# Indexer and top-k ahead of the state space mixer, and the mixer's scan done by scan instructions

## The chip, the cores and the metric

The program runs on one core of a Trainium2 chip. The metric is the device time of one execution in microseconds (us). The engines of the core work independently and wait for each other by semaphores: TensorE (PE, matmuls), VectorE (DVE), ScalarE (ACT), GpSimd (POOL) and SyncE (SP, which issues transfers).

## The reference

The program is one layer with two blocks over 512 positions of width 1024, in fp32. The change is in the first block. It projects the normed input, runs a state space mixer on one half and a sparse attention on the other, and joins them with a gated residual:

```python
def first_block(...):
    mod = silu(c) @ w_ada + b_ada
    shift, scale, gate = split(mod, 3)
    h = rms_norm(x, norm_g) * (1 + scale) + shift
    ssm_u, ssm_z, q, k, v, attn_z, q_idx, k_idx, w_idx = split(h @ w_in)
    y_ssm = s5_mixer(ssm_u, ...) * silu(ssm_z)
    y_attn = dsa_mixer(q, k, v, q_idx, k_idx, w_idx, ...) * silu(attn_z)
    return x + gate * (concat([y_ssm, y_attn]) @ w_out)

def s5_mixer(u, ...):                  # per group of 16 channels, 64 complex states
    lam_bar = exp(lam * dt)
    bu = einsum('gpc,bsgc->bsgp', b_bar, ug)
    states = associative_scan(s_t = lam_bar * s_(t-1) + bu_t)
    y = einsum('gcp,bsgp->bsgc', c_mat, states).real + d_skip * u

def dsa_mixer(q, k, v, q_idx, k_idx, w_idx, ...):
    score = sum over 8 heads of w_idx * relu(q_idx . k_idx), causal
    keep the 128 best keys of each query, attend to them with softmax
```

## The kernel before

All products of fp32 matrices are made from two parts, a rounded one and its rest. ScalarE casts a weight chunk (`whi`, L145), VectorE subtracts to get the rest (`wlo`, L146), and TensorE makes three matmuls (L153, L154, L155). Intermediate tiles of 128x512 come from one ring of 49 buffers, so that a tile's first write waits until the tile that had the buffer before is done with.

TensorE and SP run in the order of the code. The orders of VectorE, ScalarE and GpSimd are set by a scheduler. Two work streams are woven on TensorE: a main stream says after each step how many microseconds of other work it wants beside it, and `weave` (L230) draws that much from a fill stream of projections. `alongside` runs several streams by their asked times, `both` runs them one after the other, `hold(t)` only asks for t.

The stretch that the change rebuilds runs from about 70 us to about 294 us, and has two weaves (L693 and L694). In the first, the main stream is the position bias table, the tables of the state space mixer (`ssm_tables`: powers of the transition, the input matrices `Bb` and `BP`), `ssm_back` (L1201 to L1206, the output matrices F, four quarters of real and imaginary part, 24 GpSimd instructions of 128x512), `ssm_taps` (L1224 and L1225, eight groups of small matmuls, which give `We` and the tap matrix KK) and `ssm_scan`. The fill begins with the indexer's projection: four chains of 24 matmuls with 384 columns, each of which writes two tiles that VectorE splits (`iq`, L887), then the projections of queries, keys, values and the attention's gate (`ga`, L687).

`ssm_scan` works on chunks of 8 positions. 64 pairs of small matmuls (L1243) give the chunks' inputs, ScalarE copies them to `Str` and `Sti` (L1245), and then GpSimd walks the chunks: 7 steps over 16x8 chunk states at once, 7 steps over 16, 7 steps over 16x7, each of 8 instructions (L1256 to L1263), 168 in all. Beside it eight transfers put KK into the matrix `TO`, which GpSimd has cleared before (L1215).

In the second weave the index scores are made (24 pairs of matmuls, L943 and L944, relu on ScalarE, sums on VectorE at L948 and L950) and the top-k masks (48 rounds on VectorE, L966 and L967); after a hold of 40 the bias is turned (L932) and `ssm_out` makes the mixer's output in 32 groups (L1289 with `TO`, then L1291 with F and `Str`, `Sti`, all of 64 columns); after a hold of 44 `gate_sums` multiplies the 16 chunks of the gate's weights on GpSimd (`wadag`, L902), sums them on ScalarE (L903) and adds the parts on VectorE (L905, L906). The attention follows; its first TensorE work is the transposes of the keys `kn`.

Of the kernel before, what the change touches and what calls it, by code (L numbers as in the profile page):

```python
# [8 lines left out]
F32 = mybir.dt.float32  # L9
# [3 lines left out]
OP = mybir.AluOpType  # L13
# [91 lines left out]
class Kern:  # L105
# [342 lines left out]
    def block1(self):  # L448
# [235 lines left out]
        def ev_ga(j, p):  # L684
# [118 lines left out]
        self.resid(y, A["w_out"], lambda: self.gate, A["xT"], self.col("attn_norm"), (0, 1, 4, 5, 2, 6, 3, 7))  # L803
# [88 lines left out]
    def gate_sums(self):  # L892
# [4 lines left out]
        for j in range(8):  # L897
# [6 lines left out]
            yield 1.5  # L904
        nc.vector.tensor_tensor(out=self.gate, in0=part[:, 0], in1=part[:, 1], op=OP.add)  # L905
        nc.vector.tensor_tensor(out=self.gate, in0=self.gate, in1=self.col("b_ada")[:, 16:24], op=OP.add)  # L906

# [194 lines left out]
    def ssm_tables(self):  # L1102
# [6 lines left out]
        Q = [mk("q8" + x, (128, 8, 16)) for x in "ri"]  # L1109
# [25 lines left out]
        def powers(v, one, rev):  # L1135

            at = lambda e, n: [x[:, one - e - n + 1:one - e + 1] if rev else x[:, one + e:one + e + n] for x in v]
# [26 lines left out]
        yield from self.abreast(powers(PW, 7, 1), coef())  # L1164
# [3 lines left out]
        for x in range(2):  # L1168
            nc.vector.tensor_copy(Q[x][:, 0, :], PW[x][:, 0, :])
        self.Q = Q  # L1170
# [4 lines left out]
        yield from self.abreast(powers(Q, 0, 0), self.cmul(nc.vector, Bb[0], Bb[1], kb, B, tb))  # L1175
# [10 lines left out]
        self.BP = BP  # L1186

    def ssm_back(self):
# [19 lines left out]
        yield 0.0  # L1208

    def ssm_taps(self):  # L1210
# [3 lines left out]
        self.TO = TO = big.tile([128, 8, 16, 32], F32, name="TO", tag="TO", bufs=1)  # L1214
        nc.gpsimd.memset(TO.rearrange("p a b c -> p (a b c)"), 0.0)  # L1215
# [17 lines left out]
    def ssm_scan(self):  # L1233
        nc, big = self.nc, self.sp
# [598 lines left out]
```

## Time and profile before

| | before |
|---|---|
| median of 3 runs | 1275.62 us (1275.29 to 1276.29) |
| the profiled execution | 1278.79 us |
| its span, first to last instruction | 1277.0 us |
| TensorE busy | 1199.1 us (94%) |
| VectorE busy | 828.2 us (65%) |
| ScalarE busy | 558.1 us (44%) |
| GpSimd busy | 473.0 us (37%) |
| mean granted TensorE clock | 0.952 |

The profile shows one execution. Times in the trace count from the start of the span. A line such as "L146" is a line of the kernel. "PE ps_t L1291 <- POOL Str L1259: 6.6, 1, 6.6" is read: TensorE's instruction of line 1291 waited 6.6 us in all, once, and what released it was GpSimd's instruction of line 1259 that wrote `Str`. The granted clock is given as a share of full speed: 1.00 is 2.4 GHz, 0.50 is 1.2 GHz. A duration of a matmul includes its way through the array, so the distance from one start to the next is its cost in a dense stretch.

### The profile page before, as it was taken

How to read it: one execution, taken by the hardware profiler on the slowest of the kernel's cores; microseconds unless marked ns; L12 is line 12 of the kernel's file. 1: busy time of each engine (PE TensorE's matmuls, PEld its weight loads, DVE VectorE, ACT ScalarE, POOL GpSimd, SP SyncE). 2: the span in 40 equal slices, each digit the busy share in tenths (PEclk: the TensorE clock that was granted, in tenths of full speed). 3: DMA queues.
4: the chain of work that ended last, by engine and by line, in shares of the span. 5: the costliest groups of instructions: out<-in, count | busy, mean ns of one | idle time of the engine just before them, and what ended most of it. 6: DMA issues, size and time to landing. Idle time of an engine off the chain costs nothing.

```text
span 1277.0 us, 17205 instructions
## 1 busy us (share of the span) xinstructions
PE 1199.1 (94%) x6264; PEld 980.0 (77%) x6264; DVE 828.2 (65%) x1603; ACT 558.1 (44%) x1053; POOL 473.0 (37%) x612
## 2 busy tenths in 40 slices
PE   2687997999799999998999999999999999999998
PEld 2477996887578998987777777688888888888876
DVE  7986699827765456786767575554577743577731
ACT  4333542326673443655665555423544421344420
POOL 3569799517742027245666565201000000000000
PEclk9795998559999999999999999999999999999999
DMA  9442224123125442232111101134332223333230
GB/s 352 138 139 78 71 71 153 58 62 120 34 66 193 147 120 61 67 100 64 37 33 51 33 34 34 50 100 148 99 99 86 92 91 95 99 92 89 95 112 33
DMA packets 113908, 118.06 MB, mean 92 GB/s; under 512 B 16312, under 2 KB 101344, under 8 KB 113824
## 3 DMA queue, kind: packets, MB, share of 16 engines
q1 hardware_dynamic: 101280, 103.00, 25.5%
q10 hardware_dynamic: 12544, 13.96, 3.4%
q8 instruction: 49, 0.80, 0.3%
q14 instruction: 35, 0.29, 0.1%
HBM read 109.47 MB, written 6.30 MB: 91 GB/s over the span
## 4 chain that ended last, share of the span: by engine, by line
PE 74%; POOL 8%; DVE 5%; issue 3%; ACT 1%; POOLq 0%; DVEq 0%; ACTq 0%
PE ps_g L153 19%; PE ps_g L154 18%; PE ps_g L155 18%; PE ps_t L369 4%; PE ps_o L383 4%; PE ps_t L1291 3%; PE ps_s L342 2%; PE ps_s L341 2%; PE ps_t L1289 1%; DVE rb L1550 1%; POOL Sti L1263 1%; PE ps_o L1625 1%; POOL sm L1257 1%; POOL Str L1259 1%; POOL sm L1261 1%
## 5 line engine op out<-in xcount | busy, mean ns | idle before, releaser
L146 DVE TENSOR_TENSOR wlo<-wraw,whi 128x1024 fp32r<-128x1024 f32 (+4 forms) x143 | 195.6, 1373 | 71.4 <-ACT whi L145 71.2
L145 ACT CAST whi<-wraw 128x1024 fp32r<-128x1024 f32 (+4 forms) x161 | 161.7, 1010 | 175.2 <-PE ps_g L154 152.5
L153 PE MATMUL ps_g<-hT,whi 128*128 128x512 f32 x504 | 206.8, 410 | 0.0
L155 PE MATMUL ps_g<-hT,wlo 128*128 128x512 f32 x504 | 198.9, 395 | 0.0
L154 PE MATMUL ps_g<-hT,whi 128*128 128x512 f32 x504 | 198.7, 394 | 0.0
L350 POOL TENSOR_TENSOR P<-P,rsum 128x256 f32<-128x256 f32 (+3 forms) x144 | 100.8, 730 | 76.7 <-DVE rsum L1412 31.3
L345 ACT ACTIVATE P<-P,nm 128x128 f32<-128x128 f32 (+3 forms) x160 | 89.7, 561 | 75.2 <-DVE nm L343 74.2
L153 PEld LDWEIGHTS ps_g<-hT,whi 128*128 128x128 f32 x504 | 95.3, 189 | 26.9 <-issue 9.3
L155 PEld LDWEIGHTS ps_g<-hT,wlo 128*128 128x128 f32 x504 | 94.9, 188 | 22.1
L154 PEld LDWEIGHTS ps_g<-hT,whi 128*128 128x128 f32 x504 | 95.3, 189 | 18.7 <-issue 1.2
L343 DVE CUSTOM_DVE_ANT_0 P<-ps_s,att 128x128 f32<-128x128 f32 (+3 forms) x128 | 62.1, 485 | 50.9 <-PE ps_t L369 27.5
L369 PE MATMUL ps_t<-consts,P 128*128 128x128 f32 x400 | 66.1, 279 | 10.5 <-DVE qst L890 6.1
L153 PE MATMUL ps_g<-act,whi 128*128 128x512 f32 (+1 forms) x176 | 71.0, 404 | 0.0
L155 PE MATMUL ps_g<-act,wlo 128*128 128x512 f32 (+1 forms) x176 | 69.4, 394 | 0.0
L154 PE MATMUL ps_g<-act,whi 128*128 128x512 f32 (+1 forms) x176 | 69.4, 394 | 0.0
L850 POOL TENSOR_TENSOR acc<-acc,sq 128x512 f32<-128x512 f32 x15 | 21.9, 1461 | 122.1 <-ACT sq L849 119.0
L369 PEld LDWEIGHTS ps_t<-consts,P 128*128 128x128 f32 x400 | 46.7, 141 | 26.5 <-issue 14.7
L154 PE MATMUL ps_g<-wlo,hT 128*128 128x256 f32 (+1 forms) x208 | 59.3, 285 | 2.0 <-DVE wlo L146 2.0
L153 PE MATMUL ps_g<-whi,hTh 128*128 128x256 f32 x192 | 59.5, 310 | 1.3 <-ACT V L673 1.3
L153 PE MATMUL ps_g<-whi,hT 128*128 128x256 f32 (+1 forms) x208 | 59.4, 286 | 1.3 <-ACT sq L1327 1.3
L155 PE MATMUL ps_g<-whi,hT 128*128 128x256 f32 (+1 forms) x208 | 59.2, 285 | 0.0
L1739 DVE TENSOR_TENSOR conv<-ps_g,R 128x512 f32<-128x512 f32 x43 | 29.7, 692 | 43.8 <-PE ps_g L155 43.8
(487 smaller groups left out, 3031.4 us busy)
## 6 DMA issues: line engine op xcount, KB each, us to landing
wraw<-in_w_in_dram SPq DMA_DIRECT2D x56, 512.0 KB, 3.5
wraw<-in_w_up_dram SPq DMA_DIRECT2D x40, 512.0 KB, 3.5
wada<-in_w_ada_dram SPq DMA_DIRECT2D x16, 512.0 KB, 7.5
wraw<-in_w_down_dram SPq DMA_DIRECT2D x16, 512.0 KB, 3.3
wadag<-in_w_ada_dram ACTq DMA_DIRECT2D x16, 256.0 KB, 3.4
wraw<-in_w_out_dram SPq DMA_DIRECT2D x8, 512.0 KB, 3.3
wraw<-in_w_attn_br_dram SPq DMA_DIRECT2D x8, 512.0 KB, 3.3
wraw<-in_w_o_dram SPq DMA_DIRECT2D x8, 512.0 KB, 3.4
```

The lines of the kernel that those rows point to most:

```text
L145: nc.scalar.copy(hi, src)
L146: (eng or nc.vector).tensor_tensor(out=lo, in0=src, in1=hi, op=OP.subtract)
L153: mm(out, lhsT=l[0], rhs=r[0], start=start, stop=False)
L154: mm(out, lhsT=l[0], rhs=r[1], start=False, stop=False)
L155: mm(out, lhsT=l[1], rhs=r[0], start=False, stop=stop)
L343: nc.vector.tensor_tensor_reduce(out=P[i], in0=s, in1=madd(i), scale=-1.0, scalar=3.0e38, op0=OP.add, op1=OP.min, accum_out=nm[:, i:i + 1])
L345: nc.scalar.activation(P[i], P[i], AF.Exp, scale=-1.0, bias=nm[:, i:i + 1], accum_out=sums[:, i:i + 1])
L350: nc.gpsimd.tensor_tensor(out=P[n], in0=P[n], in1=sc[:, n:n + 1].to_broadcast([128, (n + 1) * 128]), op=OP.mult)
L369: nc.tensor.transpose(pt[:, o:o + 128], P[i][:, j * 128:(j + 1) * 128], self.ident)
L383: nc.tensor.matmul(acc[x * 64:(x + 1) * 64, j * 128:], lhsT=V(j), rhs=tiles[b][:, o:o + w], start=start and j == 0, stop=stop and j == 2)
L1291: nc.tensor.matmul(o, lhsT=self.F[x][a // 4][s, a % 4 * 128:(a % 4 + 1) * 128], rhs=self.St[x][s, a, 0:64], start=False, stop=x == 1)
L1739: TT(out=u, in0=p, in1=R[0], op=OP.mult)
```

## The change

The indexer alone is now the fill of the first weave, whose main stream is the bias table and the mixer's tables. The second weave starts the index scores at once, by rows of queries from the shortest on (first all heads with 256 keys, then 384, then 512), followed by the top-k; beside it stand `ssm_taps` and `ssm_scan` after a hold of 2, and after a hold of 26 more the bias and `ssm_out`.

The scan's recurrence is turned by the phase of each state, so that what is left is a real decay: GpSimd turns the inputs (12 instructions of 128x512 for two halves), VectorE runs four scan instructions of 128x512 (L1297), and GpSimd turns back (12 more). The tables for this, `turn` and `keep`, are made on GpSimd behind `BP` by six doublings with a small correction each; the power table Q on VectorE is gone. `ssm_back`, the clearing of `TO` and its eight transfers stand behind the scan now. The two additions of the gate sum are made where the residual uses the gate.

```diff
-        fill = self.both(indexer(), proj(1024, qf), proj(1536, kf), self.gemm_tn(hT, 8, w_in, 2048, 512, ev_v),
+        fill = self.both(proj(1024, qf), proj(1536, kf), self.gemm_tn(hT, 8, w_in, 2048, 512, ev_v),
...
-        self.weave(self.both(self.bias_table(), self.alongside(ssm_chunks(), tables), self.ssm_back(), self.ssm_taps(), self.ssm_scan()), fill, left=True)
+        self.weave(self.both(self.bias_table(), self.alongside(ssm_chunks(), tables)), indexer())
         self.weave(self.alongside(self.both(self.index_scores(iq, kk, wi, score), self.top_mask(score, sel)),
-                                  self.both(self.hold(40.0), self.bias_flip(), self.ssm_out(z)), self.both(self.hold(44.0), self.gate_sums())), fill, left=True)
+                                  self.both(self.hold(2.0), self.ssm_taps(), self.ssm_scan(), self.hold(26.0), self.bias_flip(), self.ssm_out(z)),
+                                  self.both(self.hold(44.0), self.gate_sums())), fill, left=True)
...
-        self.resid(y, A["w_out"], lambda: self.gate, A["xT"], self.col("attn_norm"), (0, 1, 4, 5, 2, 6, 3, 7))
+        self.resid(y, A["w_out"], self.gate_columns, A["xT"], self.col("attn_norm"), (0, 1, 4, 5, 2, 6, 3, 7))
...
+    def gate_columns(self):
+        nc, part = self.nc, self.gate_parts
         nc.vector.tensor_tensor(out=self.gate, in0=part[:, 0], in1=part[:, 1], op=OP.add)
         nc.vector.tensor_tensor(out=self.gate, in0=self.gate, in1=self.col("b_ada")[:, 16:24], op=OP.add)
+        return self.gate
...
-        for h in range(8):
-            for i in (3, 2, 1):
+        for i in (1, 2, 3):
+            for h in range(8):
...
-        Q = [mk("q8" + x, (128, 8, 16)) for x in "ri"]
...
+        PTT = nc.gpsimd.tensor_tensor
+        cur = [cs, sn]
+        for n in range(3):
...
+            PTT(out=rho[n % 2], in0=er if n == 0 else rho[1 - n % 2], in1=er if n == 0 else rho[1 - n % 2], op=OP.mult)
+        tab = big.tile([128, 3, 16, 64], F32, name="turn", tag="TO", bufs=1)
+        self.turn, self.keep = [tab[:, x] for x in range(2)], tab[:, 2]
...
+        tw = [self.pg("tw").rearrange("p (a k) -> p a k", a=16) for _ in range(2)]
+        n = 1
+        while n < 64:
+
+            g = [v[:, :, n - 1] for v in self.turn]
+            PTT(out=t1, in0=g[0], in1=g[0], op=OP.mult)
...
+            f = [v[:, :, n - 1:n].to_broadcast([128, 16, n]) for v in self.turn]
+            yield from self.cmul(nc.gpsimd, *[v[:, :, n:2 * n] for v in self.turn], f, [v[:, :, 0:n] for v in self.turn], [v[:, :, 0:n] for v in tw], 0.0)
+            n *= 2
...
-        self.TO = TO = big.tile([128, 8, 16, 32], F32, name="TO", tag="TO", bufs=1)
-        nc.gpsimd.memset(TO.rearrange("p a b c -> p (a b c)"), 0.0)
...
+                E.append(self.pg("E"))
+                nc.scalar.copy(E[x], p)
                 yield 0.6
+            c, s = (flat(v[:, a0:a0 + 8]) for v in self.turn)
+            t = [self.pg("rot") for _ in range(4)]
+            PTT(out=t[0], in0=c, in1=E[0], op=OP.mult)
+            PTT(out=t[1], in0=s, in1=E[1], op=OP.mult)
+            PTT(out=t[0], in0=t[0], in1=t[1], op=OP.add)
...
+            for x in range(2):
+                nc.vector.tensor_tensor_scan(E[x], flat(self.keep[:, a0:a0 + 8]), t[2 * x], 0.0, OP.mult, OP.add)
+            PTT(out=t[0], in0=c, in1=E[0], op=OP.mult)
+            PTT(out=t[1], in0=s, in1=E[1], op=OP.mult)
+            PTT(out=St[0][:, a0:a0 + 8, 1:65], in0=wide(t[0]), in1=wide(t[1]), op=OP.subtract)
...
         self.St = St
+        self.ssm_back()
+        self.TO = self.sp.tile([128, 8, 16, 32], F32, name="TO", tag="TO", bufs=1)
+        nc.gpsimd.memset(self.TO.rearrange("p a b c -> p (a b c)"), 0.0)
         for r in range(8):
             nc.scalar.dma_start(self.TO[0:128 - r * 16, 7 - r], self.KK[r * 16:128])
-        eng = nc.gpsimd
...
-        for i in range(1, 8):
-            step(l8, [w[:, :, :, i - 1] for w in v], [w[:, :, :, i] for w in v], m)
-        l64 = [Q[x][:, 7, :] for x in range(2)]
-        for b in range(1, 8):
-            step(l64, [w[:, :, b - 1, 7] for w in v], [w[:, :, b, 7] for w in v], [w[:, :, 0] for w in m])
```

Two places show how the orders of the engines move. The first is VectorE where the indexer's first chains are split (`iq`) amid the building of BP. Before:

```order
L1061 TENSOR_TENSOR tb<-ki,ssm 128x256
L887 TENSOR_TENSOR iq<-ps_g,iq 64x384
L1063 TENSOR_TENSOR Bb<-tb 128x256
L1061 TENSOR_TENSOR t_725<-kpwr,Bb 128x512
L1061 TENSOR_TENSOR t_726<-kpwi,Bb 128x512
L887 TENSOR_TENSOR iq<-ps_g,iq 64x384
L1063 TENSOR_TENSOR BPr<-t_725,t_726 128x512
```

After, where the lines have moved on by one at `iq` and by six in BP:

```order
L1069 TENSOR_TENSOR Bb<-tb 128x256
L1067 TENSOR_TENSOR t_685<-kpwi,Bb 128x512
L1069 TENSOR_TENSOR BPr<-t_684,t_685 128x512
L1067 TENSOR_TENSOR t_686<-kpwr,Bb 128x512
L1067 TENSOR_TENSOR t_687<-kpwi,Bb 128x512
L146 TENSOR_TENSOR wlo<-wraw,whi 128x1024
L888 TENSOR_TENSOR iq<-ps_g,iq 64x384
L1067 TENSOR_TENSOR t_684<-kpwr,Bb 128x512
L1067 TENSOR_TENSOR t_685<-kpwi,Bb 128x512
L1069 TENSOR_TENSOR BPi<-t_686,t_687 128x512
L888 TENSOR_TENSOR iq<-ps_g,iq 64x384
```

Both splits of the first chain's result (the two `iq` rows) have moved behind several multiplications of BP and one weight split.

The second is GpSimd at the end of the scan. Before, where `sm` is the scan's scratch:

```order
L1262 TENSOR_TENSOR Sti<-Sti,sm_1163 128x16x7
L1261 TENSOR_TENSOR sm_1164<-kq8i,Str 128x16x7
L1263 TENSOR_TENSOR Sti<-Sti,sm_1164 128x16x7
L902 TENSOR_TENSOR wadag<-wadag,cB 128x512 x16
L717 TENSOR_TENSOR qn<-qk,rs 128x128 x4
```

After, where `rot` is a turned input or state, and the numbers behind F tell its quarter (1447 to 1450 and 1451 to 1454 are the four quarters of Fr and Fi):

```order
L1300 TENSOR_TENSOR Str<-rot 128x8x64
L1303 TENSOR_TENSOR Sti<-rot 128x8x64
L1307 MEMSET TO 128x4096
L903 TENSOR_TENSOR wadag<-wadag,cB 128x512
L1242 TENSOR_TENSOR Fi_1451<-t_1455,t_1456 128x512
L903 TENSOR_TENSOR wadag<-wadag,cB 128x512
L1237 TENSOR_TENSOR t_1455<-kpwr,ssm 128x512
L1238 TENSOR_TENSOR t_1456<-kpwi,ssm 128x512
L1239 TENSOR_TENSOR Fr_1448<-t_1455,t_1456 128x512
L1240 TENSOR_TENSOR t_1455<-kpwr,ssm 128x512
L1241 TENSOR_TENSOR t_1456<-kpwi,ssm 128x512
L903 TENSOR_TENSOR wadag<-wadag,cB 128x512 x2
```

The clearing of `TO` and the last nineteen of F's 24 instructions now stand behind the scan, with the gate's products among them; the first five stand within it.

## Rows read from the trace of the kernel before

**Rows 1.** The page's second part: busy tenths and granted clock in 40 slices.

```profile
PE   2687997999799999998999999999999999999998
...
PEclk9795998559999999999999999999999999999999
```

**Rows 2.** Stretches: length; PE, PEld, DVE, ACT, POOL busy us (count); clock, DMA share, GB/s.

```profile
100.00:110.00 10.00, 6.44 (x27) 6.23 (x26) 9.06 (x7) 1.75 (x2) 9.77 (x6) 0.50 0.17 52
...
150.00:160.00 10.00, 10.00 (x78) 9.75 (x76) 10.00 (x16) 6.14 (x16) 10.00 (x12) 1.00 0.18 56
210.00:220.00 10.00, 2.98 (x15) 2.18 (x14) 10.00 (x1) 0.59 (x1) 9.92 (x25) 0.74 0.21 78
230.00:240.00 10.00, 10.00 (x40) 8.83 (x39) 9.62 (x25) 3.77 (x11) 10.00 (x9) 0.50 0.24 79
320.00:350.00 30.00, 23.66 (x129) 18.20 (x130) 22.01 (x47) 20.03 (x46) 21.84 (x37) 0.94 0.11 36
```

**Rows 3.** TensorE's waits, 76 to 294 us: who, for whom, total us, times, longest.

```profile
PE ps_t L1291 <- POOL Str L1259: 6.6, 1, 6.6
PE ps_g L153 <- DVE iq L887: 5.6, 2, 3.6
PE ps_g L155 <- DVE wlo L146: 2.1, 1, 2.1
```

**Rows 4.** TensorE in order of time: start us, duration us, line, tiles, shape.

```profile
87.77 0.41 PE L153 MATMUL ps_g<-hTh,whi 128*128 128x384 f32 x1 [2.06 <-DVE iq L887]
...
127.87 0.27 PE L1224 MATMUL ps_t<-consts,BPr 128*128 128x128 f32 x1
...
128.98 0.36 PE L153 MATMUL ps_g<-whi,hTh 128*128 128x256 f32 x1
...
129.41 0.29 PE L153 MATMUL ps_g<-whi,hTh 128*128 128x256 f32 x1
129.53 0.28 PE L154 MATMUL ps_g<-wlo,hTh 128*128 128x256 f32 x1
...
278.10 0.69 PE L1289 MATMUL ps_t<-U,TO 128*128 128x64 f32 x2
...
279.77 0.79 PE L153 MATMUL ps_g<-hTh,whi 128*128 128x512 f32 x1
...
283.72 0.39 PE L154 MATMUL ps_g<-hTl,whi 128*128 128x512 f32 x1
283.95 0.40 PE L155 MATMUL ps_g<-hTh,wlo 128*128 128x512 f32 x1
...
293.99 0.60 PE L735 MATMUL ps_t<-consts,kn 128*128 128x128 f32 x4
```

**Rows 5.** GpSimd in order of time: start us, duration us, idle before.

```profile
101.19 1.59 POOL L1063 TENSOR_TENSOR BPi<-t,t 128x512 f32<-128x512 f32 x1
...
110.05 1.10 POOL L1205 TENSOR_TENSOR t<-kpwi,ssm 128x512 f32<-128x512 f32 x1
...
136.69 0.48 POOL L1256 TENSOR_TENSOR sm<-kq8r,Str 128x128 f32<-128x128 f32 x1 [7.85 <-ACT Str L1245]
...
221.00 20.91 POOL L902 TENSOR_TENSOR wadag<-wadag,cB 128x512 f32<-128x512 f32 x16
```

**Rows 6.** GpSimd by line, 76 to 294 us: total busy us, mean ns.

```profile
L1215 POOL MEMSET TO<- 128x4096 f32 x1 | 3.5, 3521 | 0.7 <-PE ps_s L154 0.7
```

**Rows 7.** VectorE in order of time: start us, duration us.

```profile
91.66 2.28 DVE L146 TENSOR_TENSOR wlo<-wraw,whi 128x1024 fp32r<-128x1024 f32 x1
...
177.06 5.12 DVE L146 TENSOR_TENSOR wlo<-wraw,whi 128x1024 fp32r<-128x1024 f32 x1
...
203.46 17.25 DVE L146 TENSOR_TENSOR wlo<-wraw,whi 128x1024 fp32r<-128x1024 f32 x1
```

**Rows 8.** VectorE by line, 76 to 294 us: total busy us, mean ns.

```profile
L1061 DVE TENSOR_TENSOR t<-kpwi,Bb 128x512 f32<-128x512 f32 x4 | 6.4, 1590 | 0.0
...
L950 DVE SCALAR_TENSOR_TENSOR score<-relu,wi,score 128x512 f32<-128x512 f32 x7 | 7.0, 1003 | 0.0
```

More of the change, by code (lines that the diff above doesn't have):

```diff
@@ L1108, in ssm_tables @@
         PW = [mk("pw" + x, (128, 9, 16)) for x in "ri"]
-        Q = [mk("q8" + x, (128, 8, 16)) for x in "ri"]
+        ph = [[mk("ph%d%s" % (n, x)) for x in "ri"] for n in range(2)]
+        rho = [mk("rho%d" % n) for n in range(2)]
         tm = [mk("tm%d" % i, (128, 4, 16)) for i in range(4)]
@@ L1133, in ssm_tables, with powers @@
         yield 0.12
-        def powers(v, one, rev):
-            at = lambda e, n: [x[:, one - e - n + 1:one - e + 1] if rev else x[:, one + e:one + e + n] for x in v]
+        def powers(v, one):
+            at = lambda e, n: [x[:, one - e - n + 1:one - e + 1] for x in v]
             for n in (1, 2, 4):
@@ L1162, in coef @@
             yield 0.12
-        yield from self.abreast(powers(PW, 7, 1), coef())
+        yield from self.abreast(powers(PW, 7), coef())
         self.PW = PW
         yield None
-        for x in range(2):
-            nc.vector.tensor_copy(Q[x][:, 0, :], PW[x][:, 0, :])
-        self.Q = Q
         B = self.Bm
@@ L1174, in ssm_tables @@
         kb = [v[:, :, None].to_broadcast([128, 16, 16]) for v in (kr, ki)]
[L1175 removed]
+        yield from self.cmul(nc.vector, Bb[0], Bb[1], kb, B, tb)
         BP = [self.pages("BP" + x, 4) for x in "ri"]
@@ L1234, in ssm_scan @@
         nc, big = self.nc, self.sp
+        PTT = nc.gpsimd.tensor_tensor
         St = [big.tile([128, 16, 65], F32, name="St" + x, tag="St" + x, bufs=1) for x in "ri"]
+        flat = lambda v: v.rearrange("p a k -> p (a k)")
+        wide = lambda v: v.rearrange("p (a k) -> p a k", k=64)
         for x in range(2):
             nc.gpsimd.memset(St[x][:, :, 0:1], 0.0)
-            for a0 in (0, 8):
+        for a0 in (0, 8):
+            E = []
+            for x in range(2):
                 p = self.ps((128, 512), "t")
@@ new lines, in ssm_scan @@
+            PTT(out=t[1], in0=s, in1=E[1], op=OP.mult)
+            PTT(out=t[0], in0=t[0], in1=t[1], op=OP.add)
+            PTT(out=t[2], in0=c, in1=E[1], op=OP.mult)
+            PTT(out=t[3], in0=s, in1=E[0], op=OP.mult)
+            PTT(out=t[2], in0=t[2], in1=t[3], op=OP.subtract)
+            for x in range(2):
+                nc.vector.tensor_tensor_scan(E[x], flat(self.keep[:, a0:a0 + 8]), t[2 * x], 0.0, OP.mult, OP.add)
+            PTT(out=t[0], in0=c, in1=E[0], op=OP.mult)
+            PTT(out=t[1], in0=s, in1=E[1], op=OP.mult)
@@ L1247, in ssm_scan @@
+            PTT(out=St[0][:, a0:a0 + 8, 1:65], in0=wide(t[0]), in1=wide(t[1]), op=OP.subtract)
+            PTT(out=t[2], in0=c, in1=E[1], op=OP.mult)
+            PTT(out=t[3], in0=s, in1=E[0], op=OP.mult)
+            self.scanned = PTT(out=St[1][:, a0:a0 + 8, 1:65], in0=wide(t[2]), in1=wide(t[3]), op=OP.add)
         self.St = St
+        self.ssm_back()
+        self.TO = self.sp.tile([128, 8, 16, 32], F32, name="TO", tag="TO", bufs=1)
+        nc.gpsimd.memset(self.TO.rearrange("p a b c -> p (a b c)"), 0.0)
@@ L1248, in ssm_scan @@
         for r in range(8):
             nc.scalar.dma_start(self.TO[0:128 - r * 16, 7 - r], self.KK[r * 16:128])
-        eng = nc.gpsimd
-        v = [St[x][:, :, 1:65].rearrange("p a (b i) -> p a b i", i=8) for x in range(2)]
-        Q = self.Q
-        m = [big.tile([128, 16, 8], F32, name="sm" + x, tag="sm" + x, bufs=1) for x in "12"]
-        def step(lam, prev, cur, tmp):
-            eng.tensor_tensor(out=tmp[0], in0=lam[0], in1=prev[0], op=OP.mult)
-            eng.tensor_tensor(out=tmp[1], in0=lam[1], in1=prev[1], op=OP.mult)
-            eng.tensor_tensor(out=cur[0], in0=cur[0], in1=tmp[0], op=OP.add)
-            eng.tensor_tensor(out=cur[0], in0=cur[0], in1=tmp[1], op=OP.subtract)
-            eng.tensor_tensor(out=tmp[0], in0=lam[0], in1=prev[1], op=OP.mult)
-            eng.tensor_tensor(out=tmp[1], in0=lam[1], in1=prev[0], op=OP.mult)
-            eng.tensor_tensor(out=cur[1], in0=cur[1], in1=tmp[0], op=OP.add)
-            return eng.tensor_tensor(out=cur[1], in0=cur[1], in1=tmp[1], op=OP.add)
```

22 lines of the change are left out of this document (16 added, 6 removed).

## The prediction

> **What bounds the kernel now.** I read the 40 slices first [rows 1]. A slice is 32 us. The reader is to see two things: behind the first eleven slices TensorE is at nine tenths or more in all but one, with the clock at nine or more, so the attention and the second block are bound by TensorE's own work; and within the first nine the clock dips twice, to 5. So the change can only gain in its own stretch, and what it gains is read from one event: the first transposes of the attention, at 293.99 us [rows 4]. Every microsecond by which they come earlier comes off the end, less the TensorE work that is left for later.
>
> The stretches [rows 2] then show where TensorE loses time before that event. At 100 to 110 us it is busy for 6.44 us, at half clock. At 210 to 220 us it is busy for 2.98 us, and the clock has fallen; at 230 to 240 it is busy all the time, at 0.50. The waits [rows 3] name the causes: 6.6 us for the scan's `Str`, 5.6 us in two waits for `iq`, 2.1 for a weight split. Behind the first stands one VectorE instruction: a split that took 17.25 us, from 203.46 us on [rows 7], while GpSimd ran the scan's narrow instructions, which began at 136.69 and ended as the gate's products began at 221.00 [rows 5]. So the scan, 84 us of GpSimd, held both TensorE's next step and VectorE. The clock came back only in the dense 512-column matmuls behind `ssm_out`, which are 0.23 us apart at 283.72 [rows 4].
>
> **The prices of TensorE's work.** From one start to the next [rows 4]: a 256-column matmul 0.12 us and a 512-column one 0.23 at full clock, so 0.175 for 384 columns (in proportion); a group of taps 1.11 (127.87 to 128.98); a group of `ssm_out` 1.67 at half clock (278.10 to 279.77), so 0.83 at full clock, which no row shows.
>
> **Part one: the indexer first.** The new order of VectorE puts the first chain's second split behind 1.6 us multiplications of BP and a weight split of 2.28 us [rows 7, 8]: from `Bb` (about 83 to 85) six instructions of some 1.6, one of 2.28, two of 0.55, in all 13 us, so `iq` is ready at about 97. TensorE's third chain waits for its ring of buffers until then; before it began at 87.77 [rows 4]. That is a new wait of about 10 us, at a place where TensorE was anyhow busy little more than half. Chains three and four, 48 matmuls, take 8.4 us at full and 17 at half clock; the second dip of the clock is certain here, its length is not, and I take 15: the indexer ends at 112 (bounds 106 and 116). Before, some groups of taps were done by then; now all are to do.
>
> **Part two: scores, taps, scan.** Up to the first half of the scan TensorE has 99 matmuls of 256 columns (11.9), eight groups of taps (8.9), eight score pairs each of 256 and 384 columns and two of 512 (1.9 + 2.8 + 0.9), and 32 small ones (about 1): 27 us at full clock, and 3 for waits. The turned inputs can start at 112 + 30 = 142 (bounds 133 and 155). Behind BP, whose last GpSimd instruction ends at 102.8 [rows 5], GpSimd makes the turn tables: 36 small ones for the corrections and 30 for the doublings, of which the last six are of 512 elements (6 x 1.3) and the others between 0.2 and 0.7; I estimate 25 us, to 128. One relu waits for a ring buffer of these tables, and TensorE behind it; it comes up about 130, so it costs nothing, or 5 us where the indexer is early. Q's removal and the two additions of the gate sum are on a VectorE that TensorE doesn't wait for there: nothing.
>
> **Part three: what GpSimd does then.** The 168 instructions are gone; 24 turns, 24 for F, 14 of the gate's products stand between the turned inputs and the last quarter of F, 62 of 128x512. Their price is between 1.10 (an F product with a quiet VectorE) and 1.59 (BP beside VectorE) [rows 5]; I take the 16 products of 20.91 us, 1.31 each [rows 5], which are of the same shape and ran beside the top-k: 81 us. Clearing `TO` is 3.5 [rows 6], now on this path, and the four scan instructions, not in the trace, I put at a two-input 128x512 VectorE instruction, 1.0 us [rows 8], up to 2.3 with contention [rows 7]; two of them are not covered: 3. On VectorE they wait for GpSimd in the middle of the top-k, whose rounds and the weight splits stand behind them; GpSimd in turn stops when it needs the result, so a scan instruction can be held up by the 7 turns that GpSimd has ahead of that point at most (9 us). So `TO` can be filled from 142 + 3 + 29 x 1.31 + 3.5 = 187, some 4 us with its transfers, and the last quarter of F is ready at 142 + 3 + 81 + 3.5 = 229.5.
>
> **Part four: ssm_out.** TensorE has another 10 us of scores and 41 of projections (336 matmuls of 0.12 and the bias) before `ssm_out`: it comes there at 193, `TO` at 191. That is 20 us earlier than before and without the long stall. But the second group of four needs quarter two of F at 201, the 17th group quarter three (27 instructions behind `TO`, at 222), the 21st the last, at 229.5. At full clock TensorE would be through by 223, so it waits; I expect these waits to bring the clock down, as it was down behind the 6.6 us wait [rows 2, 3]. At half clock `ssm_out` and its 30 fill matmuls take 53 + 6: 252. By the last F: 229.5 + 12 x 1.67 + 3 = 252.5. Both agree.
>
> **The sum.** Behind it stand 72 matmuls of 256 columns (8.6) and 27 of 512 (6.3), the first of them at half clock (1.5 more): the attention starts at 268.5, 25.5 us earlier. About 30 matmuls of 512 columns, 7 us, which stood ahead of its start, now stand behind. TensorE has idle time there to put them in (busy 23.66 of 30 us from 320 on [rows 2]), so they cost between 0 and 7, and I take 5. Net 20.5. The profiled execution took 1278.8, with 1.8 around its span, and would take 1258.3; the median of the runs is 3.2 lower, so the forecast is 1275.6 - 20.5 = 1255.
>
> **A rule of the Trainium skill.** The split of 17.25 us ran beside the scan's narrow instructions, of which the first took 0.48 us [rows 5], the one of 2.28 beside the 512-element ones of BP [rows 7]. The Trainium skill (SBUF — State Buffer, section "SBUF: two separate sides") says that a VectorE instruction with two SBUF inputs and a GpSimd instruction that reads SBUF exclude each other for one instruction. By that rule the split would have waited half a microsecond; the row shows seventeen, so the measurement decides that many GpSimd instructions passed. By the rule each scan instruction would wait 1.3 us at most and the sum stays.
>
> **Rivals.**
> *All at full clock (0.2).* GpSimd runs at 1.10 and TensorE's waits in `ssm_out` are short. Then the last F is at 142 + 3 + 68 + 3.5 = 216.5, `ssm_out` ends at 12 x 0.83 + 1 = 227.5 or 193 + 30, the attention starts at 242: 52 - 7 = 45 us, 1230 (here I take the 7 whole). For it: no narrow GpSimd instructions are left in this stretch. Against it: GpSimd ran at 1.3 beside the top-k, which is denser now.
> *The gain is lost in front (0.15).* The starved splits move with the tables: four weight splits stand beside the turn's doublings, at 5.12 each instead of 1.5 [rows 7], 14 us later with all that follows: 20.5 - 14 = 6.5, 1269. For it: the doublings of 8 and 16 wide are as narrow as the scan's. Against it: they last 8 us in all.
> *Slower (0.12).* GpSimd becomes the bound of the stretch: at 1.59 each, and from 155 on, the last F is at 155 + 4 + 99 + 3.5 = 261.5, and with 23 for 12 groups at half clock and 16 behind them the attention starts at 301: 7 later, 5 moved, 1288. It decides where the last F comes after 294 - 5 - 39 = 250, 20 us later than I say. For it: F, the clearing and the gate's products all moved behind the scan. Against: the scan's 84 us became 24 x 1.31 = 31.
> *The forecast (0.53)*: 1255, from 1242 to 1266.
>
> **How the numbers follow.** A measurement of this kernel tells about 0.2% (2.5 us) from no change. Faster: 0.53 + 0.2 and most of the third rival, 0.82 with a part taken off for a smaller gain; within: 0.06; slower: 0.12. The range leaves out the slower case and the edge of the fast one: 1228 to 1273.
>
> **What would show it.** Right: TensorE's third chain starts at about 97; no split above 6 us; the turned inputs start about 142; the last Fi ends near 230; `ssm_out` runs from about 193 to 252 at 0.50; the attention's first transposes come at about 270. Wrong: `ssm_out` at full clock (then nearer 1230); the last F beyond 250; or a VectorE instruction of over 10 us beside the doublings, or the scan instructions far above 2.3.

## The result, and the profile after

The changed kernel took 1287.71 us (median of 4 runs, 1287.03 to 1288.08), the kernel before beside it 1275.95 us (1275.29 to 1279.05). The ratio is 1.0087, with a 95% interval of 1.0069 to 1.0104: slower by 0.9%, 11.8 us. The forecast was 1255, and the range ended at 1273. The profiled execution has a span of 1285.2 us, 8.2 more than before (that of the kernel before was 3.2 us above its median); the readings below explain these 8.2 and the 28.7 by which they miss the 20.5 of the forecast.

The 40 slices of the changed kernel, busy tenths of TensorE and its granted clock:

```profile
PE   2668978999999999998999999999999999999998
...
PEclk9788997579999999998999999999999999999999
```

Beside [rows 1] (32 us a slice): the dip of the clock in the fourth slice, 96 to 128 us, is gone (8 for 5), and TensorE's hole in the seventh is smaller (8 for 7). But the third slice, 64 to 96 us, has fallen from eight tenths to six, and the sixth, 160 to 192 us, from nine to seven. The clock of the eighth, 224 to 256 us, is at 5 as before; in the ninth it is at 7 for 5.

Stretches of the changed kernel, with the columns of [rows 2]:

```profile
100.00:110.00 10.00, 8.28 (x44) 8.08 (x42) 5.08 (x7) 2.22 (x6) 8.87 (x29) 0.92 0.01 2
150.00:160.00 10.00, 10.00 (x82) 9.76 (x81) 9.83 (x22) 4.20 (x11) 10.00 (x7) 1.00 0.00 1
170.00:180.00 10.00, 5.09 (x31) 4.89 (x30) 10.00 (x19) 1.98 (x6) 8.84 (x6) 0.84 0.33 105
200.00:210.00 10.00, 5.92 (x26) 4.62 (x27) 9.90 (x21) 4.13 (x13) 9.24 (x8) 0.66 0.30 105
230.00:240.00 10.00, 10.00 (x38) 8.71 (x38) 0.00 (x0) 0.78 (x3) 9.22 (x8) 0.50 0.24 70
320.00:350.00 30.00, 27.90 (x154) 20.04 (x153) 19.23 (x47) 19.36 (x47) 17.30 (x33) 0.94 0.14 46
```

The hole at 210 to 220 us is closed, and the stretch at 100 to 110 runs at 0.92 instead of 0.50. But two new holes stand at 170 to 180 and 200 to 210, both where VectorE is busy 9.9 to 10.0 of 10 us, and VectorE has nothing at all to do from 230 to 263. TensorE's waits name the holes (76 to 310 us, columns as in [rows 3]):

```profile
PE ps_g L153 <- DVE iq L888: 11.9, 1, 11.9
PE ps_g L153 <- ACT sq L662: 7.3, 3, 4.9
PE ps_g L153 <- ACT V L673: 5.8, 1, 5.8
```

The wait for `Str` is gone, and so are the narrow GpSimd instructions and the long split: by line, 76 to 294 us, VectorE's splits now take 1.5 us in the mean and 2.1 at most, where they took 2.6 in the mean before and 17.25 for one [rows 7], and the four scan instructions 1.9:

```profile
L146 DVE TENSOR_TENSOR wlo<-wraw,whi 128x1024 fp32r<-128x1024 f32 x21 | 31.3, 1499 | 28.3 <-ACT whi L145 28.2
...
L1297 DVE TENSOR_TENSOR_SCAN E<-turn,rot 128x512 f32<-128x512 f32 x4 | 7.6, 1903 | 0.0
```

GpSimd in order of time, as in [rows 5 and 6]: the first turned input, the clearing of `TO`, a wait, and the last quarter of F.

```profile
142.59 1.28 POOL L1290 TENSOR_TENSOR rot<-turn,E 128x512 f32<-128x512 f32 x1 [7.53 <-ACT E L1286]
...
189.66 3.53 POOL L1307 MEMSET TO<- 128x4096 f32 x1
...
230.55 2.49 POOL L903 TENSOR_TENSOR wadag<-wadag,cB 128x512 f32<-128x512 f32 x2 [6.21 <-DMA wadag<-in_w_ada_dram]
...
240.17 1.27 POOL L1242 TENSOR_TENSOR Fi<-t,t 128x512 f32<-128x512 f32 x1
```

And TensorE in order of time, as in [rows 4]: the first two groups of `ssm_out` and the last, and the attention's first transposes.

```profile
214.51 0.54 PE L1325 MATMUL ps_t<-U,TO 128*128 128x64 f32 x2
...
215.56 0.65 PE L1325 MATMUL ps_t<-U,TO 128*128 128x64 f32 x2
...
270.48 0.69 PE L1325 MATMUL ps_t<-U,TO 128*128 128x64 f32 x2
...
289.29 0.60 PE L736 MATMUL ps_t<-consts,kn 128*128 128x128 f32 x4
```

The attention starts 4.7 us earlier than before (289.29 for 293.99), not 25.5. The rest of the program is 12.9 us longer. The account of TensorE on both sides of that event, as stretches of the kernel before and of the changed one (from the start to the first transpose, and from there to the end):

```profile
0.00:293.99 293.99, 238.93 (x1344) 210.04 (x1344) 224.66 (x446) 108.32 (x207) 193.64 (x266) 0.80 0.38 126
293.99:1277.00 983.01, 960.19 (x4922) 769.96 (x4920) 603.50 (x1158) 449.81 (x847) 279.39 (x346) 1.00 0.27 82
```

```profile
0.00:289.29 289.29, 225.59 (x1313) 198.13 (x1314) 209.28 (x428) 106.66 (x205) 191.76 (x216) 0.83 0.39 127
289.29:1285.20 995.91, 972.30 (x4952) 778.81 (x4950) 601.72 (x1159) 451.60 (x849) 274.71 (x346) 0.99 0.26 82
```

Length less busy is TensorE's idle time. Ahead of the attention it was 55.1 us and is 63.7: **8.6 more, where the forecast had counted on less.** Busy time there fell by 13.3, of which 6.9 are 30 matmuls of 512 columns (0.23 each [rows 4]) that now stand behind the attention's start, and 6.4 are the rest, beside a mean clock of 0.83 instead of 0.80. Behind the start, busy time grew by 12.1: those 6.9, and 5.2 as the rest, beside a mean clock of 0.99 instead of 1.00. TensorE's busy time over the whole run is 1197.9 us, where it was 1199.1. The change took no work off the engine that bounds the kernel; it could only take away idle time and time at half clock, and it added idle time.

Where the attention ends there is a new wait. TensorE's first product of the attention's output `y` came at 382.95 us before, without a wait; it comes at 385.72 now, behind this one (289 to 400 us):

```profile
PE ps_g L153 <- ACT gt L775: 2.0, 1, 2.0
```

`gt` is a gate that is projected and activated inside the attention. Every kernel below that has the new order waits 1.7 to 2.0 us for it; the kernel before and the one with the new scan in the old order don't.

### The profile page after: what moved, and what is told of

Read it like the earlier page. It is cut to its first block, busy times and chain, and to the rows that moved or that the text cites. A ratio compares the mean times of both kernels' runs of the same rounds, so it can differ in the third digit from the quotient of the medians.

```text
span 1285.2 us, 17155 instructions
## 1 busy us (share of the span) xinstructions
PE 1197.9 (93%) x6264; PEld 976.9 (76%) x6264; DVE 811.0 (63%) x1587; ACT 558.3 (43%) x1053; POOL 466.5 (36%) x562
## 3 DMA queue, kind: packets, MB, share of 16 engines
q1 hardware_dynamic: 101280, 103.00, 25.5%
## 4 chain that ended last, share of the span: by engine, by line
PE 74%; DVE 10%; issue 2%; ACT 2%; POOL 1%; DMA 0%; SPq 0%; ACTq 0%; DVEq 0%; POOLq 0%
PE ps_g L153 19%; PE ps_g L154 19%; PE ps_g L155 19%; PE ps_o L383 4%; PE ps_t L369 3%; PE ps_t L1327 3%; PE ps_s L342 2%; PE ps_s L341 2%; DVE wlo L146 2%; PE ps_t L1325 1%; DVE rb L1586 1%; DVE score L973 1%; PE ps_o L1661 1%; DVE m L972 1%; DVE score L956 1%
## 5 line engine op out<-in xcount | busy, mean ns | idle before, releaser
L146 DVE TENSOR_TENSOR wlo<-wraw,whi 128x1024 fp32r<-128x1024 f32 (+4 forms) x143 | 174.9, 1228 | 94.8 <-ACT whi L145 93.7
L153 PE MATMUL ps_g<-whi,hTh 128*128 128x256 f32 x192 | 62.3, 325 | 15.9 <-ACT sq L662 7.3
L154 PE MATMUL ps_g<-wlo,hTh 128*128 128x256 f32 x192 | 57.6, 300 | 1.0 <-DVE wlo L146 1.0
```

Source lines behind the costliest of these rows:

```text
L146: (eng or nc.vector).tensor_tensor(out=lo, in0=src, in1=hi, op=OP.subtract)
L153: mm(out, lhsT=l[0], rhs=r[0], start=start, stop=False)
L154: mm(out, lhsT=l[0], rhs=r[1], start=False, stop=False)
```

## Experiments

In the expectations letters stand for theories; each says what its theory is. All ratios are to the kernel before, run beside.

**Each part alone.** The new order with the old scan: the kernel before, with the second weave's order and the row loops of the change.

```diff
-        fill = self.both(indexer(), proj(1024, qf), ...
-        self.weave(self.both(self.bias_table(), self.alongside(ssm_chunks(), tables), self.ssm_back(), self.ssm_taps(), self.ssm_scan()), fill, left=True)
+        fill = self.both(proj(1024, qf), ...
+        self.weave(self.both(self.bias_table(), self.alongside(ssm_chunks(), tables)), indexer())
...
+                                  self.both(self.hold(2.0), self.ssm_back(), self.ssm_taps(), self.ssm_scan(), self.hold(26.0), self.bias_flip(), self.ssm_out(z)),
...
```

> The kernel before with the new order alone: indexer first, index scores by rows of queries, top-k at once; scan by GpSimd steps, power table Q, F ahead of the taps, clearing of TO ahead of it, gate sum as before. If the order is what costs: 1285 or more. If the new scan and what moved behind it cost: below 1276. I expect 1280: GpSimd ends its 84 us of scan steps at about 225 us, 4 later than before, VectorE's splits are starved beside the top-k.

Then the new scan with the old order: the changed kernel with the old two weaves and row loops.

```diff
-        self.weave(self.both(self.bias_table(), self.alongside(ssm_chunks(), tables)), indexer())
+        self.weave(self.both(self.bias_table(), self.alongside(ssm_chunks(), tables), self.ssm_taps(), self.ssm_scan()), fill, left=True)
...
```

> The changed kernel with the old order of the two weaves (taps and scan ahead of the index scores, fill beginning with the indexer): the new scan, tables on GpSimd, F and TO behind the scan. If the order costs: TensorE is not held up by VectorE, since the scan instructions stand ahead of the top-k, and the time is below 1270. If the scan's work on GpSimd and VectorE costs wherever it stands: 1280 or more.

The order alone: 1.0133 (1.0111 to 1.0156), 1295.31 us, where I had expected 1280. TensorE waits 15.8 us for `Str` and 13.3 for `iq`; nothing runs on it from 210 to 220 us. The scan alone: 1.0141 (1.0125 to 1.0156). TensorE waits 13.8 us for relu, 11.9 for `iq`, 9.3 for `sq`, and the attention starts at 306.71. Both theories of cost hold, each by its bound. So each part alone loses more than both together (1.0087). The scan is what lets the new order do without the long wait for `Str`, and the order gives the scan room; neither brings a gain of its own.

**The q/k root's place.** ScalarE's square root for the norms of q and k (`rt`) waited 15.1 us in two pieces for VectorE in the changed kernel:

```profile
168.07 0.38 ACT L662 ACTIVATE sq<-ps_g 128x256 f32<-128x256 f32 x1 [3.01 <-DVE s L663]
175.69 0.23 ACT L278 ACTIVATE rt<-ms 128x32 f32<-128x32 f32 x1 [7.24 <-DVE ms L277]
...
202.32 0.23 ACT L278 ACTIVATE rt<-ms 128x32 f32<-128x32 f32 x1 [7.88 <-DVE ms L277]
```

Its instructions were put behind the second weave.

```diff
-            rs.append(self.rstd(s8.rearrange("p a b -> p (a b)"), 64, 32, sm, "qk%d" % n))
+            rs.append((s8, n))
...
```

> The changed kernel, but the two chains of the q and k norms' reciprocal roots (L277 to L283) stand behind the second weave instead of behind each projection. Theory A (ScalarE, in its fixed order, stands still for the first of them, 7.2 us at 168 to 176 us, and for the second, 7.9 us at 194 to 202 us, since VectorE does their first step only behind a scan instruction or behind the top-k; TensorE then lacks free accumulators): the waits of L153 for sq and V fall from 13.1 us to under 4, ssm_out starts 8 to 10 us earlier, time 1276 to 1280. Theory B (VectorE is simply full, so that whatever is taken from the front of its queue is missed later): waits elsewhere in the stretch, time within 3 us of 1287.7.

1.0050 (1.0032 to 1.0068). The wait for V falls from 5.8 to 1.1, that for `sq` stays at 7.6, and the attention starts at 286.76. The two come to 8.7, not under 4, and the time, 1285.38, lies within theory B's bounds.

**The fill inside ssm_out.** Is the half clock there a matter of the thin fill? First more fill, then none.

```diff
-                    yield 0.2
+                    yield 0.9
```

> The changed kernel with 0.9 instead of 0.2 us of other matmuls asked after every two groups of ssm_out, so that the projections that stood behind it (72 matmuls of 256 columns and some of 512) stand between its groups. If the half clock of ssm_out comes from waits ahead of it or in it, it stays at 0.50 for as long as before and the time stays within 3 us of 1287.7. If it comes from the groups' own small matmuls, the denser stretch keeps 1.00 or nearly so, ssm_out with these projections takes 45 us instead of 76, and the time is 1258 to 1270.

> The changed kernel with no other matmuls asked between the groups of ssm_out (0.0 instead of 0.2); the 30 matmuls follow it. If the groups' own matmuls bring the clock to half: the 32 groups alone keep 0.50 and take 53 to 54 us, and the 30 matmuls cost 0.12 instead of 0.21 us each at their new place: 2 to 3 us less than 1287.7. If it comes from waits: no wait stands ahead of the groups any more than in the changed kernel, so the same clock; the two are told apart by whether the fall comes in the groups with no wait ahead of it.

With 0.9: 1.0142 (1.0127 to 1.0157). Three stretches of it:

```profile
220.00:230.00 10.00, 10.00 (x55) 9.16 (x55) 9.76 (x16) 4.51 (x12) 10.00 (x8) 0.83 0.30 99
230.00:240.00 10.00, 10.00 (x42) 9.06 (x42) 3.65 (x7) 1.09 (x4) 9.69 (x9) 0.50 0.19 54
...
250.00:260.00 10.00, 10.00 (x42) 9.06 (x41) 0.00 (x0) 0.37 (x1) 0.00 (x0) 0.50 0.19 52
```

Neither expectation held. The clock stays at 1.00 for 11 us of groups, until 226.5 (in the changed kernel for 3, until 217.5), then it is at 0.50 until 277; `ssm_out` takes from 215.67 to 288, and the matmuls moved into it cost nearly twice their price (0.21 to 0.27 us from one start to the next). So more fill puts the fall off but doesn't prevent it. With 0.0 instead of 0.2: 1.0078 (1.0050 to 1.0107), no different from the changed kernel; `ssm_out` ends 5 us earlier, and the fill comes behind it. The groups alone run at 0.50, so the fill is not what brings the clock down; the 2 to 3 us expected are less than this interval could show.

**Where the idle time came from.** In the new order VectorE gets its top-k rounds early, and the reductions of q and k (`s`, L663), the scan instructions and the weight splits stand between them. ScalarE works its queue in order and stands still for `s` and `ms`, so that TensorE finds no free accumulator. If this is the cause, top-k rounds that wait for the last reduction take the `sq` waits away.

```diff
...
+            if i == 1:
+                yield 26.0
...
-                nc.vector.max(m8, a)
-                nc.vector.match_replace(out=a, in_to_replace=m8, in_values=a, imm_value=-3.0e38)
-                yield 0.37 * (i + 1)
+                with self.tc.issue_after(self.reduced.ins):
+                    nc.vector.max(m8, a)
+                    nc.vector.match_replace(out=a, in_to_replace=m8, in_values=a, imm_value=-3.0e38)
+                yield 0.18 * (i + 1)
```

> The changed kernel with the top-k rounds put behind the last reduction of the q and k projections on VectorE (L663), so that they run during ssm_out, where VectorE stood idle from 229 us on; TensorE's order is nearly the same (6 matmuls fewer ahead of the attention). Theory C (the early top-k fills VectorE, and the reductions, the scan instructions and the weight splits queue behind its rounds; ScalarE's squares and TensorE's accumulators wait for them): the waits of L153 for sq and V, 13.1 us, fall under 3, ssm_out starts at about 200 instead of 213, the attention at 276 and the time is about 1275. Theory D (GpSimd's turns slow VectorE and set the pace, top-k or not): the waits for sq stay above 6 and the time above 1284.

1.0029 (1.0013 to 1.0045). TensorE's waits, 76 to 310 us:

```profile
PE ps_g L153 <- ACT V L673: 11.8, 1, 11.8
...
PE ps_g L153 <- ACT sq L662: 0.6, 1, 0.6
```

The `sq` waits are gone, as expected; but the wait for V is 11.8 instead of 5.8, and `ssm_out` starts at 213.28, hardly earlier. Theory D is out, and of theory C the half on `sq` holds. With the late root as well:

> As topk_late, and the two chains of the norms' reciprocal roots behind the second weave as well. Theory C: 0 to 4 us less than topk_late, since the chains then wait for little. Theory D: as topk_late, within 3 us of 1285.4.

1.0030 (1.0012 to 1.0048), and the wait for V is still 11.7. So in these two kernels it isn't VectorE that holds V. ScalarE's queue in order of time, 184 to 203 us, shows what does:

```profile
185.53 1.05 ACT L145 CAST whi<-wraw 128x1024 fp32r<-128x1024 f32 x1
195.41 5.11 ACTq L1313 DMA_DIRECT2D TO<-KK  x8
...
201.81 0.62 ACT L673 COPY V<-ps_g 128x256 f32<-128x256 f32 x2
```

The eight transfers into `TO` are issued by ScalarE. They can't go before GpSimd has turned the states back and cleared `TO` (which lies in the buffer of the turn tables), at 195.4. ScalarE stands from 186.6 on, the V copies stand behind it in the queue, and TensorE behind those. A chain of GpSimd had lain just behind VectorE's.

**GpSimd issues the transfers itself.** On top of the kernel with both:

```diff
-            nc.scalar.dma_start(self.TO[0:128 - r * 16, 7 - r], self.KK[r * 16:128])
+            nc.gpsimd.dma_start(self.TO[0:128 - r * 16, 7 - r], self.KK[r * 16:128])
```

> As topk_late_rstd, but the eight transfers into TO are issued by GpSimd, behind the clearing of TO, instead of by ScalarE. Theory E (with the top-k out of the way the next wait is ScalarE's queue: its eight issues stand still for the clearing of TO, which can only come behind the turns because it has the turn tables' buffer, and take 5.1 us more, and the copies of V stand behind them, 11.7 us for TensorE at 190 to 202): the wait for V falls under 3, ssm_out starts at 203 to 206 instead of 213, limited by TO itself, and the time is 1271 to 1275. Theory F (the wait only moves, to TO or to the F that GpSimd makes later): ssm_out starts at 211 or later, 1279 or more.

1.0070 (1.0043 to 1.0097): worse, as theory F had it; of theory E only the wait for V came true. TensorE's waits, and GpSimd in order of time:

```profile
PE ps_t L1329 <- DMA TO<-KK: 4.8, 1, 4.8
PE ps_t L1331 <- POOL Fi L1246: 2.9, 1, 2.9
PE ps_g L153 <- ACT whi L145: 2.8, 1, 2.8
PE ps_g L153 <- ACT V L673: 2.5, 1, 2.5
```

```profile
199.40 4.37 POOL L1313 DMA_DIRECT2D TO<-KK  x8
...
207.14 11.04 POOL L904 TENSOR_TENSOR wadag<-wadag,cB 128x512 f32<-128x512 f32 x9
218.15 1.31 POOL L1243 TENSOR_TENSOR Fr<-t,t 128x512 f32<-128x512 f32 x1
```

V is nearly free, and the waits are for `TO` and F now. The transfers go out only at 199.4, behind the last instruction of a quarter of F and two gate products, and nine more gate products stand in a row within the next quarter of F, ahead of its first sum. The variant without fill in `ssm_out` came out the same, 1.0071 (1.0047 to 1.0095):

> to_pool with ssm_out as in out_bare: 2 to 3 us less than to_pool, about 1270, which would be 5 us below the kernel before.

**GpSimd in the order in which TensorE needs it.** Transfers right behind the clearing, then all of F, the gate products last.

```diff
         self.St = St
-        self.ssm_back()
...
+        self.ssm_back()
...
-                with self.tc.issue_after(self.scanned.ins):
+                with self.tc.issue_after(self.backed.ins):
```

where `backed` is the last instruction of F. This was run with the late top-k and root, and on the changed kernel alone:

> Late top-k and late q/k roots, and GpSimd's work in another order: TO is cleared, its eight transfers are issued by GpSimd at once, then all eight halves of F are made, and only then the sixteen gate products. Theory G (three chains reach ssm_out within some ten us of each other: ScalarE's queue, TO, F; with all three cleared TensorE starts where its own work ends): no V wait over 3 us, no wait for F, the first product of ssm_out at 202 to 206 (212.95 with late top-k and late roots alone), attention's first transpose at 276 to 280, a time of 1270 to 1276, as fast as the kernel before or a little faster. Rival H (TensorE's own work before ssm_out is what takes until 211, and the waits only change places): the first product at 210 or later, the first transpose at 285 or later, 1279 or more.

> GpSimd's and ScalarE's new order alone, on the changed kernel, with the top-k left early. Theory G: the sq waits of 7.3 us stay, the V wait falls from 5.8 to under 3, the first product of ssm_out at 209 to 212 (214.51 in the changed kernel), attention's first transpose at 284 to 287, a time of 1282 to 1285. Rival H: the same start as in the changed kernel, 1286 to 1289.

With the late top-k 1.0026 (1.0012 to 1.0040): `ssm_out` starts at 205.77 and the attention at 283.82, with no wait for V or F and one of 6.7 us for `TO`. The start came as theory G said, the attention some 4 us and the end 5 us later than it said. On the changed kernel alone 1.0041 (1.0024 to 1.0058), `ssm_out` at 208.24, 0.8 earlier than it said, the attention at 285.12 and the time within its bounds. This last kernel also answers the question whether waits bring the clock down. Three of its stretches:

```profile
200.00:210.00 10.00, 10.00 (x59) 7.88 (x59) 9.96 (x21) 3.06 (x7) 9.61 (x9) 1.00 0.84 242
210.00:220.00 10.00, 10.00 (x45) 8.85 (x46) 9.56 (x21) 0.00 (x0) 9.61 (x9) 0.66 0.02 8
220.00:230.00 10.00, 10.00 (x39) 8.76 (x38) 9.24 (x20) 1.99 (x5) 9.92 (x9) 0.50 0.20 73
```

TensorE is busy without a break from 180 us on, its clock is at 1.00 as `ssm_out` begins, and in it the clock falls to 0.50 all the same.

**And the first wait, for iq.** On top of the kernel with all three, VectorE makes `iq` ahead of most of BP.

```diff
-            yield from self.cmul(nc.vector if q < 2 else nc.gpsimd, ..., 0.62 if q < 2 else 0.0)
+            yield from self.cmul(nc.vector if q < 2 else nc.gpsimd, ..., 3.2 if q < 2 else 0.0)
```

> As the kernel with GpSimd's new order, and VectorE makes iq before most of its products for BP (the cost given to a product of BP is raised from 0.62 to 3.2, so the indexer's instructions stand ahead). Theory G (what comes first anywhere in the chain up to the scan moves the whole chain): TensorE's wait for iq falls from 11.9 us to 3 to 6, the first turned input starts at 136 to 139 (142.05), the first product of ssm_out at 200 to 203 (205.77), attention's first transpose at 278 to 281 (283.82), and the time is 1276 to 1278.5. Rival T (GpSimd's turn tables, which end at 134.9, hold back a relu and with it the scores, the taps and the scan): the wait for iq falls, and a wait for relu of 4 us or more takes its place; the first turned input at 141 or later, 1280 to 1282.

0.9998 (0.9987 to 1.0008): 1276.52 us, as fast as the kernel before. Its waits, 76 to 310 us, and TensorE's account up to the attention and behind it:

```profile
PE ps_s L950 <- ACT relu L953: 8.8, 1, 8.8
PE ps_t L1329 <- DMA TO<-KK: 6.4, 1, 6.4
...
PE ps_g L153 <- DVE iq L889: 3.2, 1, 3.2
```

```profile
0.00:277.45 277.45, 221.74 (x1307) 195.35 (x1308) 220.32 (x428) 106.98 (x204) 198.81 (x224) 0.83 0.40 131
277.45:1272.70 995.25, 972.15 (x4958) 778.63 (x4956) 603.71 (x1160) 451.36 (x849) 274.41 (x346) 0.99 0.26 82
```

Both theories saw something: the first turned input started at 138.40 (136 to 139 expected), the wait for `iq` fell from 11.9 to 3.2, and one of 8.8 for relu came up, not for the turn tables but for a buffer that the delayed BP holds. The sum still fell, the first product of `ssm_out` came at 202.10 (200 to 203 expected), and the attention starts 16.5 us earlier than before. TensorE's idle time up to there is 55.7 us, back at the 55.1 of the kernel before.

The series, with TensorE's waits for these ahead of `ssm_out` and in it (us). Each profile shows one execution (that of the late top-k took 1285.12 us, where the median of its runs is 1280.48), so starts and ratios don't go together to the microsecond:

| kernel | iq | sq | V | TO | F | ssm_out starts | attention starts | ratio |
|---|---|---|---|---|---|---|---|---|
| changed | 11.9 | 7.3 | 5.8 | | | 214.51 | 289.29 | 1.0087 |
| top-k late | 11.8 | 0.6 | 11.8 | | | 213.28 | 286.88 | 1.0029 |
| and root late | 11.9 | 0.6 | 11.7 | | | 212.95 | 286.32 | 1.0030 |
| and GpSimd issues | 11.8 | 0.6 | 2.5 | 4.8 | 2.9 | 211.26 | 289.78 | 1.0070 |
| and GpSimd's order | 11.9 | 0.6 | | 6.7 | | 205.77 | 283.82 | 1.0026 |
| and iq first | 3.2, relu 8.8 | 1.1 | | 6.4 | | 202.10 | 277.45 | 0.9998 |
| GpSimd's order on the changed kernel | 11.8 | 7.3 | | | | 208.24 | 285.12 | 1.0041 |

The waits are not a sum: whichever is taken away, the next stands a few microseconds behind. Three queues (VectorE's, ScalarE's, GpSimd's) reach `ssm_out` within some ten microseconds of each other: the late top-k moves its start by 1.2 us, GpSimd's order alone by 6.3, all of them by 12.4. `TO` in a buffer of its own, which would free its clearing from the turns, was not tried. No kernel here beats the kernel before.

## Why the prediction was wrong

**Right, to the microsecond or nearly.** Part one: one wait for `iq` of 11.9 us, until 97.5 (about 10 us, until 97). Part two: the first turned input at 142.59 (142), which is part luck: the indexer ended at 107.9 (112), and the way from there took 34.7 us (30). The tables end at 135.1, 7 later than I said, and TensorE's wait for relu is 0.5. The scan instructions took 1.58 to 2.31 (1.0 to 2.3). No split is starved any more. `ssm_out` with its fill took 57.6 us (59), nearly all of it at 0.50.

**The step that failed is part four: "it comes there at 193".** I counted 51 us of TensorE work from 142 on and no wait. It took 71.9 (142.59 to 214.51): 13.2 idle and 58.8 busy. The idle time is `sq` and V, 7.3 and 5.8, which I had put at nothing. I had named the cause in part three, the scan instructions "in the middle of the top-k, whose rounds and the weight splits stand behind them", and then asked only what this does to GpSimd. TensorE's projections need ScalarE to empty their accumulators, ScalarE needs VectorE's reductions, and VectorE was busy for 9.9 of each 10 us there. The experiments show it: with the late top-k `sq` falls to 0.6, and V, whose copies stood on ScalarE behind the root's wait until 202.3, falls to 1.1 with the late root and to nothing with GpSimd's order alone, where a V copy stands ahead of the root. The busy time is 7.8 more than the 51 because the count was wrong too. There are 378 matmuls of 256 columns, not 336; behind `ssm_out` stand the 72 that I expected, so most of the 42 were in no term of mine (5.0 at 0.12 each). From one start to the next the 378 cost 50.6, 0.134 each, since the clock fell behind the waits (0.84 at 170 to 180, 0.66 at 200 to 210). The "10 us of scores" went the other way: at my own price twelve matmuls of 512 columns are 2.8, and with the 90 small ones of the scan, which I had left out, they took 5.8.

**Part three was too low as well, and would have been the next bound.** From 142.59 to the clearing GpSimd needed 47.1 us for 29 instructions, 1.62 each with its short waits, not 1.31. `TO` was cleared at 193.2 (187), and its transfers stood on ScalarE's queue ahead of the V copies, a queue that part four didn't look at; there they ended at 198.3, ahead of the root. The last F was ready at 241.4 (229.5), and nobody waited for it, since `ssm_out` itself was 21.5 late.

**The half clock had the right length and the wrong cause.** I expected waits to bring it. In the kernel with GpSimd's order alone there is none, and the clock falls from 1.00 to 0.50 within the groups; with no fill it falls as well, and with more fill later. What in the groups does it isn't separated: their matmuls are of 64 columns, and two thirds of them use 64 rows. The rival *All at full clock* was therefore out in every kernel run here. Its price was off as well: a group took 1.05 at full clock (214.51 to 215.56), not 0.83.

**The sum.** The moved matmuls were taken at 5, between 0 and 7. 30 is the right count, but the rest of the run is 12.9 us longer. The idle time that was to hide them [rows 2] did not: TensorE is idle 23.6 us behind the attention's start, 22.8 before; up to the first product of `y` it was 8.5 and is 7.5, of which 2.0 are the new wait for `gt`. So the upper end, 6.9, was due whole, and 5.2 came on top, beyond the bound. Part of it shows in the second block, which the change doesn't touch: one more wait of 1.3 us for `sq` at 522, and a clock of 0.66 at 587 to 597 us, where the same work before, at 580 to 590, ran at 0.83, both with the same wait of 3.4 us for `cmp`. From 490 us to the end the changed kernel fell back by 4.3 us against the kernel before, the one with `iq` first by only 1.7, and yet its whole rest grew by 12.2. Why the clock behind the same waits differs stays open.

The reading of [rows 1] was off by one: behind the eleventh slice two slices, not one, are under nine tenths, the second being the last. Nothing hangs on it.

In all: 20.8 us of the miss lie ahead of the attention (4.7 for 25.5) and 7.9 behind it (12.9 for 5); together 28.7. The first part splits by the account above. The forecast implied 7 less idle time than before (13 of 20.4 since 76 us), 7 of moved work, and so 11.5 from the clock; it became 8.6 more, 6.9 and 6.4.

**The rivals.** *Slower* gave 1288, and 1287.7 was measured, but that is luck: its mechanism didn't happen. It wanted the last F beyond 250 and GpSimd as the bound. GpSimd's products held TensorE only in the experiments, when VectorE's and ScalarE's queues had been put in order. *The gain is lost in front* saw the right kind of thing in the wrong place: the splits beside the doublings are not starved (three in a row took 3.62 us, 1.2 each).

**The Trainium skill's rule** (SBUF — State Buffer, section "SBUF: two separate sides") was set against the split of 17.25 us. With the scan's narrow instructions gone, splits of the same shape take 1.5 in the mean, which bears out that it was these that held VectorE. Their number alone is not the cause: the 17.25 ran beside some forty of 128x112 and 0.42 to 0.51 us each, but beside the scan's 128x16 steps of the same kernel (184 to 203 us) two splits took 1.2, and beside the doublings it was GpSimd that waited (128x16 instructions of 0.2 us took 1.1 beside the three splits at 111 to 115 us). Why the split lost its turn in the one place stays open. Elsewhere the rule's price, one instruction, agrees with a row further down: a GpSimd product beside a split of 1.20 us took 1.13 longer than one beside none.

## What to carry to other kernels

Where one engine is busy 94% of the time, ask first whether a change takes work off that engine; if not, its gain is bounded by idle time and by time at half clock, and every instruction that is moved behind the stretch comes back at its full price. When TensorE's work up to some event is summed, follow each accumulator to the engine that empties it and that engine's queue to what it waits for, the transfers that it issues among them: a queue that stands still for one semaphore holds back everything behind it. And after a wait is taken away, look for the next chain before expecting the whole wait as gain: here three lay within ten microseconds.

## What the runs showed of the hardware

The groups of `ssm_out` come to run at 0.50 with TensorE busy 10.0 of 10 us, no wait, and the clock at 1.00 as they begin: 5 us after the first group in the kernel with GpSimd's order alone, 11 us after it with the denser fill, where the clock was back at 1.00 for 4 us (277 to 281).

GpSimd's price for one instruction goes by what VectorE does at the moment, more than by how busy it is. Two products for F of the same shape, in the kernel with GpSimd's order and the late top-k:

```profile
186.95 2.23 POOL L1245 TENSOR_TENSOR t<-kpwi,ssm 128x512 f32<-128x512 f32 x1
...
201.73 1.10 POOL L1242 TENSOR_TENSOR t<-kpwi,ssm 128x512 f32<-128x512 f32 x1
```

VectorE was busy throughout beside the first, and for 1.10 of the 1.20 us from 201.70 on beside the second. Beside the first ran a split of 1.20 us, from 187.00 on, and an `ms` of 1.09; beside the second nothing but top-k rounds. Behind the clearing F's products took 1.10 to 1.11 and its sums and differences 1.26 to 1.27, so 1.31 was too much for F there; it was too little for the turns.

Eight transfers issued in a row hold the engine that issues them: 5.11 us on ScalarE, 4.36 to 4.37 on GpSimd.
